# Gated linear attention in 128-token tiles: decays from the middle, three float32r products for states times query, states ahead of the gate, gate on feature partitions

## The chip, the cores and the metric

One core of one Trainium2 chip runs the whole program. The metric is the device time of one execution in microseconds; the kernel before was timed three times, and the median counts.

## What is computed

The reference is one inference step of a two-layer decoder: layer 0 has a recurrent mixer, layer 1 has gated linear attention (GLA); each layer then has cross-attention to a memory and an MLP. 1024 new tokens of one prompt and 8 sequences of 8 sample tokens go through it, 1088 token columns in all, everything in float32. The GLA mixer is the part that matters here. For each of 4 heads (key width 128, value width 256), with `bcum` the running sum of the log decays within a chunk:

```
q_in = qc * exp(bcum);  k_in = kc * exp(-bcum)
att  = where(mask, einsum('bthk,bshk->bhts', q_in, k_in), 0)
o    = einsum('bhts,bshv->bthv', att, vc) + einsum('bthk,bhkv->bthv', q_in, S)
k_end = kc * exp(g - bcum)
S    = exp(g) * S + einsum('bshk,bshv->bhkv', k_end, vc)
out  = (rmsnorm(o) * silu(gate)) @ w_out
```

The reference walks the prompt in chunks of 64 tokens; with another chunk length the result is the same apart from rounding. A sample sequence is one chunk of 8 tokens and starts from a given state.

## The kernel before

Activations lie transposed, features on partitions, in three column chunks c = 0, 1, 2 of 384, 384 and 320 columns (the last 64 are the samples). Each chunk has two or three 128-token tiles (`TILES`, `PTILES`). Every weight product splits both operands into a high and a low float32r part and issues three products into one PSUM bank (`mm3`, L97): that is the bulk of the program. PSUM has two banks under the name `pa`, three under `pb`, three under `pm`.

`gla` (L873) goes through the four heads one by one (L1099). `V` (L965) makes the values with tokens on partitions. Then for each chunk: `z_chain` (L930) makes the decays and their exponentials `qi`, `ki`, `ke`; `QK` (L974) makes queries and keys with features on partitions (`gemm_in`, L239) and multiplies them by those exponentials; `core_a` (L988) transposes `ke` into `kT` and makes the masked attention `att`; `G` (L1059) makes the gate with tokens on partitions (`gemm_tok`, L254); `core_b` (L1013) makes the output; `gate` (L1075) normalizes and gates it; `T` (L1086) transposes it, splits it into high and low parts and queues the output product (`gemm_out`, L266).

In `core_b` a 128-token tile holds two 64-token chunks. Each chunk has its own product of keys and values over 64 partitions (L1023), its own product of 64 queries with the state (L1030), and its own update of the state on VectorE (L1033), so that within a tile the second chunk's query product waits for the first one's update. The attention product covers the tile at once (L1027). These products are plain float32, and each stands in the trace as two TensorE instructions of 256 columns. In the last chunk the samples follow: the attention (L1040), eight query products with 32 columns of weights (L1051), eight products over 64 partitions for the new states (L1052), in pairs, with two buffers for the sample states and their loads (L1010) and stores (L1056).

The order on each engine is not the program's. A scheduler sets it when the kernel is compiled: it takes what is ready by its own clock, in order of priority, so that products of `QK` or of an output can stand between two products of `core_b`. On the chip every engine then keeps its compiled order.

## Time and profile before

| | us |
|---|---|
| three runs | 3103.0, 3103.41, 3107.08 |
| median | 3103.41 |
| profiled execution | 3104.66 |
| its span, first to last instruction | 3102.9 |
| TensorE busy in the span | 3050.6 |
| VectorE busy | 1743.2 |
| ScalarE busy | 1016.2 |

Busy time is the union of an engine's instructions. A matmul's record is longer than its turn, since matmuls are pipelined: the turn is the time from its start to the next one's start. The chain views give each piece of the path the time it held the path; the start column of a timeline gives the turns.

### The profile page before, as it was taken

How to read it: one execution, taken by the hardware profiler on the slowest of the kernel's cores; microseconds unless marked ns; L12 is line 12 of the kernel's file. 1: busy time of each engine (PE TensorE's matmuls, PEld its weight loads, DVE VectorE, ACT ScalarE, POOL GpSimd, SP SyncE). 2: the span in 40 equal slices, each digit the busy share in tenths (PEclk: the TensorE clock that was granted, in tenths of full speed). 3: DMA queues.
4: the chain of work that ended last, by engine and by line, in shares of the span. 5: the costliest groups of instructions: out<-in, count | busy, mean ns of one | idle time of the engine just before them, and what ended most of it. 6: DMA issues, size and time to landing. Idle time of an engine off the chain costs nothing.

```text
span 3102.9 us, 46542 instructions
## 1 busy us (share of the span) xinstructions
PE 3050.6 (98%) x19319; PEld 2930.7 (94%) x19319; DVE 1743.2 (56%) x3266; ACT 1016.2 (33%) x1847; POOL 193.6 (6%) x274
## 2 busy tenths in 40 slices
PE   8999999999999999999999999999999999999997
PEld 8999999989999999999889888899999999999997
DVE  7577786566444444446454454675575444444445
ACT  7555573234111211113333232442242112111114
POOL 4100020001000000001000000010010000000002
PEclk9999999999999999999999999999999999999998
DMA  8311113331111111111011102033321111111111
GB/s 271 119 43 43 42 60 103 102 113 36 54 42 42 55 42 41 46 50 43 28 57 42 57 28 70 21 98 106 126 62 55 42 41 48 48 42 41 45 51 58
DMA packets 155780, 194.85 MB, mean 63 GB/s; under 512 B 11281, under 2 KB 140561, under 8 KB 155569
## 3 DMA queue, kind: packets, MB, share of 16 engines
q1 hardware_dynamic: 152768, 182.82, 19.0%
q0 software_dynamic: 2800, 9.06, 0.8%
q8 instruction: 151, 2.47, 0.3%
q14 instruction: 61, 0.49, 0.1%
HBM read 178.34 MB, written 13.52 MB: 62 GB/s over the span
## 4 chain that ended last, share of the span: by engine, by line
PE 91%; DVE 4%; ACT 2%; DMA 2%; issue 1%; POOL 0%; SPq 0%; DVEq 0%; ACTq 0%; POOLq 0%
PE pa L101 12%; PE pa L99 12%; PE pa L100 12%; PE pb L99 9%; PE pb L100 9%; PE pb L101 9%; PE pm L99 5%; PE pm L100 5%; PE pm L101 4%; PE pa L262 2%; PE pa L264 2%; PE pa L263 2%; DVE xl L312 1%; DMA kvt<-in_cache_v 1%; PE pm L1030 1%
## 5 line engine op out<-in xcount | busy, mean ns | idle before, releaser
L100 PE MATMUL pa<-xl,whi 128*128 128x384 f32 (+2 forms) x2336 | 761.6, 326 | 2.7 <-DVE xl L312 2.7
L99 PE MATMUL pa<-xh,whi 128*128 128x384 f32 (+2 forms) x2336 | 761.5, 326 | 0.7 <-ACT xh L311 0.7
L101 PE MATMUL pa<-xh,wlo 128*128 128x384 f32 (+2 forms) x2336 | 761.9, 326 | 0.0
L279 DVE TENSOR_TENSOR x<-x,pb 128x384 f32<-128x384 f32 (+1 forms) x792 | 411.9, 528 | 206.7 <-PE pb L101 205.9
L99 PE MATMUL pb<-hh,whi 128*128 128x384 f32 (+1 forms) x1584 | 523.1, 332 | 4.5 <-DVE x L279 3.5
L100 PE MATMUL pb<-hl,whi 128*128 128x384 f32 (+1 forms) x1584 | 519.1, 328 | 0.0
L101 PE MATMUL pb<-hh,wlo 128*128 128x384 f32 (+1 forms) x1584 | 517.7, 327 | 0.0
L186 ACT CAST whi<-raw 128x1024 fp32r<-128x1024 f32 (+1 forms) x250 | 256.7, 1040 | 693.0 <-PE pa L100 349.2
L100 PEld LDWEIGHTS pa<-xl,whi 128*128 128x128 f32 x2336 | 439.3, 188 | 4.3 <-DVE xl L312 4.0
L99 PEld LDWEIGHTS pa<-xh,whi 128*128 128x128 f32 x2336 | 439.4, 188 | 2.7 <-ACT xh L311 1.0
L101 PEld LDWEIGHTS pa<-xh,wlo 128*128 128x128 f32 x2336 | 439.4, 188 | 0.6 <-DVE wlo L187 0.6
L187 DVE TENSOR_TENSOR wlo<-raw,whi 128x1024 fp32r<-128x1024 f32 (+1 forms) x250 | 303.3, 1224 | 241.0 <-ACT whi L186 240.2
L679 DVE SCALAR_TENSOR_TENSOR r<-pa,rstd 128x384 f32<-128x384 f32 (+1 forms) x192 | 102.4, 534 | 399.1 <-PE pa L101 398.4
L99 PEld LDWEIGHTS pb<-hh,whi 128*128 128x128 f32 x1584 | 297.5, 188 | 16.8 <-DVE x L279 7.2
L100 PEld LDWEIGHTS pb<-hl,whi 128*128 128x128 f32 x1584 | 298.2, 188 | 2.2 <-issue 1.6
L680 ACT ACTIVATE r<-r 128x768 f32<-128x768 f32 (+1 forms) x96 | 77.6, 808 | 674.4 <-DVE r L679 674.4
L101 PEld LDWEIGHTS pb<-hh,wlo 128*128 128x128 f32 x1584 | 298.0, 188 | 0.5 <-issue 0.4
L279 DVE TENSOR_TENSOR x<-x,pm 128x320 f32<-128x320 f32 (+1 forms) x360 | 191.0, 531 | 111.6 <-PE pm L101 111.5
L306 POOL TENSOR_TENSOR acc<-acc,sq 128x384 f32<-128x384 f32 (+1 forms) x105 | 118.8, 1132 | 2058.9 <-ACT sq L305 2040.3
L99 PE MATMUL pm<-hh,whi 128*128 128x320 f32 (+1 forms) x720 | 234.6, 326 | 0.0
L101 PE MATMUL pm<-hh,wlo 128*128 128x320 f32 (+1 forms) x720 | 234.5, 326 | 0.0
L100 PE MATMUL pm<-hl,whi 128*128 128x320 f32 (+1 forms) x720 | 234.5, 326 | 0.0
(305 smaller groups left out, 4338.7 us busy)
## 6 DMA issues: line engine op xcount, KB each, us to landing
raw<-in_mlp_w SPq DMA_DIRECT2D x128, 512.0 KB, 3.7
kvt<-in_cache_kT SPq DMA_DIRECT2D x64, 256.0 KB, 5.0
kvt<-in_cache_v SPq DMA_DIRECT2D x64, 256.0 KB, 4.8
raw<-in_xa_wv SPq DMA_DIRECT2D x16, 512.0 KB, 4.9
raw<-in_rg_w_in SPq DMA_DIRECT2D x16, 512.0 KB, 3.6
raw<-in_xa_wq SPq DMA_DIRECT2D x16, 512.0 KB, 3.4
raw<-in_xa_wo SPq DMA_DIRECT2D x16, 512.0 KB, 3.5
raw<-in_gla_w_in SPq DMA_DIRECT2D x16, 512.0 KB, 3.6
```

What stands on the lines that cost most here:

```text
L99: mm(out, lh, rh, start=first, stop=False)
L100: mm(out, lh, rl, start=False, stop=False)
L101: mm(out, ll, rh, start=False, stop=last)
L186: nc.scalar.copy(hi[:, o], raw[:, o])
L187: nc.vector.tensor_sub(lo[:, o], raw[:, o], f32(hi[:, o]))
L262: mm(out, self.xh[c][:, k, xs], hv[:, kk, :], start=k == 0, stop=False)
L263: mm(out, self.xh[c][:, k, xs], lv[:, kk, :], start=False, stop=False)
L264: mm(out, self.xl[c][:, k, xs], hv[:, kk, :], start=False, stop=k == 7)
L279: nc.vector.tensor_add(x, x, p[:, :per * w].rearrange("p (m t) -> p m t", m=per))
L306: (nc.vector if m % 4 == 3 else nc.gpsimd).tensor_add(self.acc[c][:, :w], self.acc[c][:, :w], sq[:, :w])
L679: nc.vector.scalar_tensor_tensor(r[:, f], p[f][:, :w], 0.0, self.rstd[c], op0=OP.max, op1=OP.mult)
L680: nc.scalar.activation(r, r, AF.Square)
```

## The change

A tile of 128 tokens becomes one chunk. The mask is a full lower triangle, and the prefix sums run over 128 tokens (three scans of 128 columns in place of one masked scan). The exponents of `qi` and `ki` are taken relative to the sum at the tile's 64th token; the state is multiplied by the decay up to there (`eg[:, i]`) before the query product, and by that of the whole tile (`eg[:, 4 + i]`) in its update. The query product uses high and low parts of the query (`qh`, `ql`, made in `core_a`) and of the scaled state (`sh`, `sl`), three float32r products per tile; the first tile of a head has no state and no such product. The key-value products, the state updates and the splits move to a new function `states`, which stands ahead of `G`. `G` uses `gemm_in` and so gives the gate with features on partitions; it is multiplied in behind the transposes in `T`, and `T` of the chunk before moves ahead of `G`. The samples' query products all stand ahead of their state products, and their states have four buffers, loaded at the start of the last chunk. `qi` has one buffer in place of two.

```diff
...
-            nc.vector.tensor_tensor_scan(bc[:, :pw], smask[:, :pw], m[:, :pw], 0.0, OP.mult, OP.add)
+            for t0 in range(0, pw, 128):
+                nc.vector.tensor_tensor_scan(bc[:, t0:t0 + 128], one, m[:, t0:t0 + 128], 0.0, OP.mult, OP.add)
...
+            nc.scalar.activation(eg[:, 0:n], bv[:, :, 63], AF.Exp, scale=1.0 / 16.0)
+            nc.scalar.activation(eg[:, 4:4 + n], bv[:, :, 127], AF.Exp, scale=1.0 / 16.0)
+            nc.vector.tensor_sub(view(d), bv, bv[:, :, 63:64].to_broadcast([128, n, 128]))
+            nc.scalar.activation(e[0][:, :pw], d[:, :pw], AF.Exp, scale=1.0 / 16.0)
+            nc.scalar.activation(e[1][:, :pw], d[:, :pw], AF.Exp, scale=-1.0 / 16.0)
+            d = self.t("tt", [128, MAXW], F32, 2)
+            nc.vector.tensor_sub(view(d), bv[:, :, 127:128].to_broadcast([128, n, 128]), bv)
...
+            qh = self.t("qih", [128, MAXW], R32)
+            ql = self.t("qil", [128, MAXW], R32)
+            nc.scalar.copy(qh[:, :pw], qi[:, :pw])
+            nc.vector.tensor_sub(ql[:, :pw], qi[:, :pw], f32(qh[:, :pw]))
...
-        def core_b(h, c, kT):
-            qi, ki, ke, eg = Z.pop(c)
-
-            kvs = {}
+        def states(c, kT):
+
+            eg, out = Z[c][3], []
             for i, (j, t0, tw) in enumerate(PTILES[c]):
                 if i % 2 == 0:
-                    bank = self.pa if i == 0 else self.pb
-                    two = [bank(), bank()]
-                kvs[i] = [t[:, i % 2 * 256:i % 2 * 256 + 256] for t in two]
-                for s in range(2):
-                    nc.tensor.matmul(kvs[i][s], kT[s * 64:s * 64 + 64, i, :], vo[j][s * 64:s * 64 + 64, :],
-                                     start=True, stop=True)
+                    bank = self.pb()
+                kv = bank[:, i % 2 * 256:i % 2 * 256 + 256]
+                nc.tensor.matmul(kv, kT[:, i, :], vo[j], start=True, stop=True)
+                if (c, i) == (0, 0):
+                    S["cur"] = self.t("S", [128, 256])
+                    nc.vector.tensor_copy(S["cur"], kv)
+                    out.append(None)
+                    continue
+                st = S["cur"]
+                sh, sl = self.t("Sh", [128, 256], R32, 2), self.t("Sl", [128, 256], R32, 2)
+                nc.scalar.activation(sh, st, AF.Copy, scale=eg[:, i:i + 1])
+                nc.vector.scalar_tensor_tensor(sl, st, eg[:, i:i + 1], f32(sh), op0=OP.mult, op1=OP.subtract)
+                nc.vector.scalar_tensor_tensor(st, st, eg[:, 4 + i:5 + i], kv, op0=OP.mult, op1=OP.add)
+                out.append((sh, sl))
+            return out
+
+        def core_b(h, c, kT, qh, ql, sts):
...
                 p = self.pm()
...
+                mm(o, atts[i], vo[j], start=True, stop=sts[i] is None)
+                if sts[i] is not None:
+                    sh, sl = sts[i]
+                    mm(o, qh[:, ts], sh, start=False, stop=False)
+                    mm(o, ql[:, ts], sh, start=False, stop=False)
+                    mm(o, qh[:, ts], sl, start=False, stop=True)
                 o_done(j, tw, p)
...
+            w = WID[c]
+            p = self.gemm_in(us, c)
             if c == NC - 1:
                 self.free(us)
-            return out
-
-        def gate(gss, c):
+            gt = self.t("gt", [128, 2, MAXW])
+            for f in range(2):
+                nc.vector.tensor_mul(gt[:, f, :w], p[f][:, :w], self.rstd[c])
+
+                sg = self.t("tt", [128, MAXW], F32, 2)[:, :w]
+                nc.scalar.activation(sg, gt[:, f, :w], AF.Exp, scale=-1.0)
+                nc.scalar.activation(sg, sg, AF.Ln, bias=1.0)
+                nc.scalar.activation(sg, sg, AF.Exp, scale=-1.0)
+                nc.vector.tensor_mul(gt[:, f, :w], gt[:, f, :w], sg)
+            return gt
...
-                nc.vector.scalar_tensor_tensor(vo[j][:tw], vo[j][:tw], ro[:tw, j:j + 1], gs[:tw], op0=OP.mult, op1=OP.mult)
...
+                nc.scalar.activation(vo[j][:tw], vo[j][:tw], AF.Copy, scale=ro[:tw, j:j + 1])
...
+                z = gt[:, dt, :w]
+                nc.vector.scalar_tensor_tensor(z, p[:, :w], gn, z, op0=OP.mult, op1=OP.mult)
+                nc.scalar.copy(hT[0][:, dt, :w], z)
+                nc.vector.tensor_sub(hT[1][:, dt, :w], z, f32(hT[0][:, dt, :w]))
...
-                    for b in range(0, 4, 2):
+                    for b in range(0, 8, 2):
                         load_s0(h, b)
-                kT = core_a(h, c)
+                core = core_a(h, c)
                 if c + 1 < NC:
                     z_chain(h, c + 1)
                     QK(us, h, c + 1)
                     self.tick()
+                if c:
+                    T(uo, h, c - 1, gt)
...
-                gss = G(ug, h, c)
+                sts = states(c, core[0])
+                gt = G(ug, h, c)
                 self.tick()
-                core_b(h, c, kT)
-                gate(gss, c)
+                core_b(h, c, *core, sts)
+                gate(c)
...
```

## Rows read from the trace of the kernel before

**Rows 1.** The page: busy us, share of the span and instructions of each engine.
```profile
PE 3050.6 (98%) x19319; PEld 2930.7 (94%) x19319; DVE 1743.2 (56%) x3266; ACT 1016.2 (33%) x1847; POOL 193.6 (6%) x274
```

**Rows 2.** GLA stretch: window, us, then busy us of PE, PEld, DVE, ACT, POOL; clock, DMA.
```profile
1467.00:2035.00 568.00, 563.34 (x3635) 485.53 (x3634) 296.50 (x655) 199.82 (x490) 35.82 (x49) 1.00 0.16 47
```

**Rows 3.** The longest wait of TensorE there: waiter, releaser, total us, times, longest.
```profile
PE pm L1030 <- DVE S L1033: 1.7, 3, 0.6
```

**Rows 4.** The chain that ended last in that stretch, shares of 568 us by line.
```profile
by line: PE pa L262 11.7%; PE pa L264 11.3%; PE pa L263 11.2%; PE pb L99 11.2%; PE pb L100 10.6%; PE pb L101 10.4%; PE pm L1030 5.0%; PE pa L1023 3.9%; PE pm L1027 3.2%; PE pa L1051 2.4%; PE pm L1052 1.8%; PE pm L938 1.7%; PE pm L995 1.7%;
```

**Rows 5.** The chain in one chunk's core: start us, us, what.
```profile
1541.64 0.84 PE pa L1023 x3
1542.48 0.11 PE pb L1023
...
1542.70 0.43 PE pb L1023 x3
1543.13 0.63 PE pm L1027 x2
1543.76 1.06 PE pa L1023 x4
...
1546.46 0.58 PE pm L1030 x2
1547.04 0.35 PE pb L99
```

**Rows 6.** Timeline of TensorE, float32r products, 256 columns, then 384: start us first.
```profile
1540.28 0.28 PE L264 MATMUL pa<-whi,xl 128*128 128x256 f32 x1
1540.40 0.28 PE L262 MATMUL pa<-whi,xh 128*128 128x256 f32 x1
...
1515.10 0.33 PE L99 MATMUL pb<-xh,whi 128*128 128x384 f32 x1
1515.28 0.33 PE L100 MATMUL pb<-xl,whi 128*128 128x384 f32 x1
1515.45 0.33 PE L101 MATMUL pb<-xh,wlo 128*128 128x384 f32 x1
```

**Rows 7.** Timeline of TensorE, float32 transposes among float32r products: start us first.
```profile
1607.69 0.28 PE L262 MATMUL pa<-whi,xh 128*128 128x256 f32 x1
1607.81 0.49 PE L1092 MATMUL pm<-ident,vo 128*128 128x128 f32 x3
1608.06 0.42 PE L100 MATMUL pb<-hl,whi 128*128 128x384 f32 x1
1608.32 0.34 PE L101 MATMUL pb<-hh,wlo 128*128 128x384 f32 x1
```

**Rows 8.** The chain in the sample part of the last head: start us, us, what.
```profile
2015.86 1.84 PE pa L1051 x8
2017.70 1.49 PE pm L1052 x6
...
2020.28 1.06 PE pm L1052 x4
...
2025.08 0.98 PE pa L1051 x4
```

**Rows 9.** VectorE and ScalarE in the stretch by line and shape: busy us, mean ns.
```profile
L1069 DVE SCALAR_TENSOR_TENSOR gs<-pa,rtok,gs 128x256 f32<-128x256 f32 x32 | 15.4, 483 | 43.2 <-ACT gs L1068 42.9
L1084 DVE SCALAR_TENSOR_TENSOR vo<-vo,oro,gs 128x256 f32<-128x256 f32 x32 | 15.2, 527 | 0.1
L1095 DVE SCALAR_TENSOR_TENSOR hl<-pm,vec,hh 128x384 fp32r<-128x384 f32 x16 | 9.9, 618 | 12.1 <-ACT hh L1094 12.1
L950 DVE TENSOR_TENSOR_SCAN tt<-smask,ki 128x384 f32<-128x384 f32 x8 | 7.7, 957 | 0.3
L957 DVE TENSOR_TENSOR tt<-tt 128x384 f32<-128x384 f32 x8 | 4.5, 558 | 0.3
L960 ACT ACTIVATE qi<-tt 128x384 f32<-128x384 f32 x8 | 4.1, 508 | 0.0
```

More of the change, by code (lines that the diff above doesn't have):

```diff
@@ L877, in gla @@
         w_in = a.gla_w_in[0]
-        smask = self.t("smask", [128, MAXW])
-        nc.gpsimd.memset(smask, 1.0)
-        nc.gpsimd.memset(smask.rearrange("p (n t) -> p n t", t=64)[:, :, 0], 0.0)
+        one = self.t("one", [128, 128])
+        nc.gpsimd.memset(one, 1.0)
         smask8 = self.t("smask8", [128, 64])
@@ L884, in gla @@
         nc.gpsimd.memset(smask8.rearrange("p (n t) -> p n t", t=8)[:, :, 0], 0.0)
-        ones = self.t("tt", [128, MAXW], F32, 2)[:, :128]
-        nc.gpsimd.memset(ones, 1.0)
         tri = self.t("tt", [128, MAXW], F32, 2)[:, :128]
-        nc.gpsimd.affine_select(tri, ones, pattern=[[1, 128]], compare_op=OP.is_ge, fill=0.0, base=0, channel_multiplier=-1)
-        nc.gpsimd.memset(tri[0:64, 64:128], 0.0)
+        nc.gpsimd.affine_select(tri, one, pattern=[[1, 128]], compare_op=OP.is_ge, fill=0.0, base=0, channel_multiplier=-1)
         pmask = self.t("pmask", [128, 128], U8)
@@ L894, in gla @@
         blk = self.t("blk", [64, 8])
-        nc.gpsimd.affine_select(blk, ones[:64, :8], pattern=[[-8, 8]], compare_op=OP.is_ge, fill=0.0, base=0, channel_multiplier=1)
+        nc.gpsimd.affine_select(blk, one[:64, :8], pattern=[[-8, 8]], compare_op=OP.is_ge, fill=0.0, base=0, channel_multiplier=1)
         nc.gpsimd.affine_select(blk, blk, pattern=[[8, 8]], compare_op=OP.is_ge, fill=0.0, base=7, channel_multiplier=-1)
@@ L916, in gla @@
         ro = self.t("oro", [128, 9])
-        ntok = self.t("ntok", [128, 9])
         def a_lo(c):
@@ L954, in z_chain @@
             d = self.t("tt", [128, MAXW], F32, 2)
-            for t0, n, L, g0 in ((0, PRO[c] // 64, 64, 0),) + (((256, 8, 8, 4),) if c == NC - 1 else ()):
-                bv = bc[:, t0:t0 + n * L].rearrange("p (n t) -> p n t", t=L)
-                nc.vector.tensor_sub(d[:, t0:t0 + n * L].rearrange("p (n t) -> p n t", t=L),
-                                     bv[:, :, L - 1:L].to_broadcast([128, n, L]), bv)
-                nc.scalar.activation(eg[:, g0:g0 + n], bv[:, :, L - 1], AF.Exp, scale=1.0 / 16.0)
@@ L960, in z_chain @@
-            nc.scalar.activation(e[0][:, :w], bc, AF.Exp, scale=1.0 / 16.0)
-            nc.scalar.activation(e[1][:, :w], bc, AF.Exp, scale=-1.0 / 16.0)
+            n = pw // 128
+            bv = bc[:, :pw].rearrange("p (n t) -> p n t", t=128)
+            view = lambda ap: ap[:, :pw].rearrange("p (n t) -> p n t", t=128)
+            nc.scalar.activation(eg[:, 0:n], bv[:, :, 63], AF.Exp, scale=1.0 / 16.0)
+            nc.scalar.activation(eg[:, 4:4 + n], bv[:, :, 127], AF.Exp, scale=1.0 / 16.0)
@@ new lines, in z_chain @@
+            nc.vector.tensor_sub(view(d), bv, bv[:, :, 63:64].to_broadcast([128, n, 128]))
[3 more added lines that the diff above has]
+            nc.vector.tensor_sub(view(d), bv[:, :, 127:128].to_broadcast([128, n, 128]), bv)
+            if c == NC - 1:
+                sv = bc[:, pw:w].rearrange("p (n t) -> p n t", t=8)
+                nc.vector.tensor_sub(d[:, pw:w].rearrange("p (n t) -> p n t", t=8), sv[:, :, 7:8].to_broadcast([128, 8, 8]), sv)
+                nc.scalar.activation(eg[:, 8:16], sv[:, :, 7], AF.Exp, scale=1.0 / 16.0)
+                nc.scalar.activation(e[0][:, pw:w], bc[:, pw:w], AF.Exp, scale=1.0 / 16.0)
+                nc.scalar.activation(e[1][:, pw:w], bc[:, pw:w], AF.Exp, scale=-1.0 / 16.0)
@@ L1038, in core_b @@
                 nc.gpsimd.dma_start(a.S_prompt[0, 0, h], S.pop("cur"))
-                po = self.pa()
-                nc.tensor.matmul(po[:64, :256], att8, vo[8][:64, :], start=True, stop=False)
+                po = self.pm()
+                mm(po[:64, :256], att8, vo[8][:64, :], start=True, stop=False)
+                for b in range(8):
+                    g = b // 4 * 32
+                    mm(po[g:g + 32, :256], qm[:, b, :], s0s[b // 2 * 2][:, b % 2, :], start=False, stop=b % 4 == 3)
                 for b in range(0, 8, 2):
-                    if b not in s0s:
-                        load_s0(h, b)
                     s0 = s0s.pop(b)
@@ L1059, in G, with gate @@
         def G(us, h, c):
-            out = []
-            for j, t0, tw in TILES[c]:
-                p = self.pa()
-                self.gemm_tok(us, c, t0, tw, p[:tw, :256])
-                gs = self.t("gs", [128, 256], F32, 3)
-                nc.scalar.activation(gs[:tw], p[:tw, :256], AF.Exp, scale=ntok[:tw, j:j + 1])
-                nc.scalar.activation(gs[:tw], gs[:tw], AF.Ln, bias=1.0)
-                nc.scalar.activation(gs[:tw], gs[:tw], AF.Exp, scale=-1.0)
-                nc.vector.scalar_tensor_tensor(gs[:tw], p[:tw, :256], self.rtok[:tw, j:j + 1], gs[:tw], op0=OP.mult, op1=OP.mult)
-                out.append(gs)
+            w = WID[c]
+            p = self.gemm_in(us, c)
             if c == NC - 1:
                 self.free(us)
-            return out
-        def gate(gss, c):
+            gt = self.t("gt", [128, 2, MAXW])
[7 more added lines that the diff above has]
+            return gt
+        def gate(c):
             j0 = TILES[c][0][0]
```

51 lines of the change are left out of this document (17 added, 34 removed).

## The prediction

> **What bounds the kernel now.** I read the page first, then the busy times of the GLA stretch, its waits, its chain, and last the timelines that give the price of one turn. TensorE is busy for 3050.6 of 3102.9 us [rows 1]. In the 568 us in which this mixer runs it is busy for 563.3 us at the full clock (1.00), while VectorE is busy for 296.5 and ScalarE for 199.8 [rows 2]: 4.7 us of TensorE's time are idle there. The waits say the same from the other side: the longest, that of the query products for the state update, is 1.7 us in total [rows 3]. So there is hardly a stall to remove. What the change can win is TensorE's own work, and the chain of the stretch shows who holds the path: the query products (L1030) 5.0% of 568 us, the key-value products (L1023) 3.9% in `pa` alone, the attention products (L1027) 3.2% [rows 4].
>
> **Prices of a turn.** A float32 pass of 256 columns: six take 1.49 us, four 1.06 [rows 8], so 0.215 us each; a run of n passes that takes up half or a quarter of the array costs 0.215 n plus 0.20 (1.06 less 4 times 0.215). The same 0.20 stands on a run of two full-array passes that comes behind half-array ones (0.63 for two L1027) [rows 5], so it is paid at each change of shape. The next float32r product behind such a run holds the path for 0.35 us instead of 0.17 [rows 5]: 0.18 for the way back. A float32r product costs 0.12 us with 256 columns and 0.173 with 384 (two starts in 0.35) [rows 6]; with 320 I put 0.147, between them.
>
> **The change part by part**, on TensorE, over four heads.
>
> - Core of the prompt. Before: L1030 28.4 us (5.0% of 568), L1023 22.2 in `pa` plus 32 passes in `pb` at 0.135 (0.11 and 0.43 for four [rows 5]), 4.3, L1027 18.2 [rows 4]: 73.1. After: the key-value products of whole tiles are 8 per head, 64 passes, at 0.215: 13.8. The attention products stay 64 passes; without the changes of shape they cost 13.8. The query products are 28 tiles with three float32r products at 0.12: 10.1. Sum 37.7, a gain of 35.4.
> - Gate. Before, 9 tiles of 24 products at 0.12: 25.9 us per head. After, 48 products in each chunk, 48 times (0.173 + 0.173 + 0.147): 23.7. Four heads: 8.8 gained. The sum counts turns alone, as all these products are full tiles of float32r.
> - Samples. The 128 passes (64 query, 64 state) stay. In the last head they stand in runs of 8, 6, 4 and 4 [rows 8], with two more; with the query products together there should be three or four. I take four runs less per head, 16 times 0.20: 3.2 gained. The loads of states b = 4 and 6, which waited for a buffer, go out with the first two; two more issues stand on SP's queue ahead of weight loads. Their cover is the last chunk's `G` (48 turns of 0.147, 7 us) and the output product popped ahead of it (8.3 us); without it a weight unit that comes late would be waited for, a few us a head at most.
> - Products between the pieces of the core. Twelve times a float32r product followed a half-array one of the core; at 0.18 [rows 5] that is 2.2 gained.
> - Waits: the 1.7 us for the state update [rows 3] go, since `states` makes all updates while `G` runs. What is late next is the third pair of `sh`, `sl`: the middle chunk needs three pairs and has buffers for two. The third is made once the first tile's products are done, in a ScalarE step of 256 columns (0.51 with 384, so some 0.42) and a VectorE step of 0.48 [rows 9] plus hand-over, some 1.2 us by estimate; the cover is the second tile (0.43 + 0.36) and the third's attention product (0.43), 1.22. I put 0.3 us a head, 1.2 in all; without any cover it would be 4.8.
> - Switches from float32 passes to float32r within a tile, 56 of them. The trace has none of two-pass products in the full array. The nearest rows are transposes among float32r products: no time is lost on the way in (0.12), and three of 128 columns with the product behind them take 0.51 us [rows 7] where 3 times 0.108 (half of 0.215) and 0.173 make 0.50. So I take 0.01 each, 0.6. The other end is the 0.20 of a change of shape: 11.
> - VectorE, per chunk of 384: scans about +0.3 (by estimate: three starts in place of one, on 0.957), one more subtraction for the exponents and one for `ql` at 0.56, two for the split in `T` at 0.56, four in `G` at 0.56 in place of three at 0.48, and three gate products of 0.53 less [rows 9]: +1.8, so some 21 us in all. ScalarE: +0.5 for `qh`, some 0.42 a tile for `sh` and again for the gate's scale, a small exponential, and six of 0.51 in `G` for nine of some 0.43 (256 columns, by estimate): +2.3, some 27 us. In a stretch of about 518 us that makes VectorE 61% and ScalarE 44% busy [rows 2]. I cost it at nothing: the cover is the 8.3 us of turns in each of `QK` and `G`. Longest is `z_chain`: with three exponentials, two VectorE steps, a scan, two subtractions and three more exponentials it takes about 7 us [rows 9], and it must be done when `QK` of the same chunk is. With the cover gone it would be paid in part twelve times (the slower rival).
> - POOL loses a memset per head and four small ones in the setup; nobody waits for them. At nothing.
> - Leftover: 1 us for waits that I do not see.
>
> Gains 35.4 + 8.8 + 3.2 + 2.2 + 1.7 = 51.3; costs 1.2 + 0.6 + 1.0 = 2.8; net 48.5. The profiled execution took 3104.66 us, its span and 1.8 us around it, which is 1.25 above the median of the runs. Against it the sum gives 3056; from the median of 3103.4 it gives 3055, which is my number.
>
> **A rule against it.** The rows of one core show key-value passes of the two halves both ways: four in line in 1.06 us, and others whose turns fall to 0.11 because two run side by side [rows 5]. Page "TensorEngine Tiling (Array Packing)" of the Trainium skill, section Key Properties, says that tiles on different parts of the array load and multiply in parallel, by which the two halves before would already cost no more than one whole product. By that rule, joining them would gain only the changes of shape. By these rows the overlap is the exception, and the chain's share is what was paid; the sum goes by it, and the rule is a rival.
>
> **The rivals.**
>
> 1. *The halves ran together.* If the path's share of L1023 holds other work's time, joining halves wins little: 26.5 us before against 13.8 after, so up to 12.7 less gain. For it: turns of 0.11; against: four passes in 1.06 [rows 5]. It gives 3068. Chance 0.08.
> 2. *Buffers give part back.* `qi`, `gt` and the split state have few buffers, `tt` two for eight uses a chunk, and `T` now stands between `QK` and `G` and needs the gate's scale first. If each of twelve chunks loses 1.5 us on this, 18 us go back: 3073. For it: more steps in series on VectorE and ScalarE; against: TensorE found 563.3 us of work in 568 [rows 2] with similar chains, since the compiled order fills gaps. Chance 0.16.
> 3. *The three products are not what they say.* If the query products ran as float32 passes, 84 of them would cost 0.43 instead of 0.12: 26 us back, 3081. Against it: the same type gives 0.12 in `V` [rows 6]. Chance 0.02.
> 4. *Slower: the single `qi` buffer puts `z_chain` on the path.* The next chunk's `qi` may be written only when attention, `qh`, `ql` and, in the last chunk, a POOL copy have read the old one. If the chain of some 7 us then begins only at the end of `QK`, its banks stay full and TensorE stands still. It decides from 48.5 / 12 = 4 us a chunk; fully exposed it is 12 times 7, 84 us: 3139. Against it: only the two last exponentials need `qi` and `ki` free, and 8.3 us of `QK` lie over the chain. Chance 0.03.
>
> **How the numbers follow.** The forecast has 0.71, with its own range 3042 to 3066: the lower end adds another 13 us, as much again as the 7 us of the smaller gains and 6 for changes of shape around other products that I did not count; the upper end takes the 11 us of switches. Rivals 1 and 2 reach to 3073, with some spread to 3078; the range 3042 to 3078 leaves out less than 2 in 10. About 0.2% (6 us) is what a measurement of this kernel can tell from no change. Faster by more than that: forecast and rivals 1 to 3, less a little for a mixture of 2 and 3 that eats nearly everything: 0.95. Within it: 0.02. Slower: 0.03.
>
> **What would show it.** Right: in the GLA stretch (then about 520 us) the chain gives the key-value, attention and state-query products together about 38 us, the state-query products turn over every 0.12 us, the gate's products stand at 0.173, and TensorE's idle time stays under some 8 us. Wrong: float32r products of the core at 0.2 or more apart (the switches), waits of TensorE for `sl`, `gt` or `qi` of more than 10 us in total (rival 2), or the query and key banks waiting for exponentials (rival 4). The prediction falls if the stretch gets shorter by less than 30 us.

## The result and the profile after

The changed kernel takes 3050.45 us (median of four runs, 3049.25 to 3050.82) beside 3105.24 for the kernel before (3103.0 to 3107.08; in the later comparisons its medians are 3103.3 to 3105.4). The ratio is 0.9823 with a 95% interval of 0.9806 to 0.984: faster by 1.8%. The forecast was 3055.0 in 3042 to 3078. The profiled execution took 3050.53 us, its span is 3048.8; against the profiled execution before (3104.66) that is a gain of 54.1 us where 48.5 were forecast.

The page of the changed kernel: busy us, share of the span and instructions of each engine, beside [rows 1].

```profile
PE 2999.3 (98%) x18923; PEld 2920.6 (96%) x18923; DVE 1752.6 (57%) x3304; ACT 1038.8 (34%) x1907; POOL 193.6 (6%) x267
```

TensorE has 51.3 us and 396 instructions less; VectorE has 9.4 us more and ScalarE 22.6 us more, and neither is near its limit.

Where it went is told by cutting the execution at the same two places in each kernel: from the start of the first value product of the GLA mixer (L262) to the start of the last transpose of its gated output. For the kernel before and then the kernel after, the windows between these places: window, us, busy us of PE, PEld, DVE, ACT, POOL; clock, DMA share and GB/s.

```profile
1466.78:2036.45 569.67, 564.80 (x3644) 486.67 (x3642) 298.17 (x659) 200.71 (x491) 36.46 (x50) 1.00 0.16 47
```

```profile
1464.88:1980.41 515.53, 511.81 (x3246) 475.06 (x3244) 308.67 (x697) 223.70 (x552) 38.74 (x42) 1.00 0.17 52
```

The stretch is 569.67 - 515.53 = 54.1 us shorter, which is the whole gain: without it the profiled executions leave 3104.66 - 569.67 and 3050.53 - 515.53, 2535.0 us each. TensorE's idle time in it is 515.53 - 511.81 = 3.7 us, 4.9 before. The granted clock is 1.00 in both, the upper of its two levels (2.4 GHz). What lies outside the stretch is untouched by the edits and still takes 2529.7 to 2535.6 us in the profiled executions, while the stretch of the same kernel run again came out at 515.51. So the experiments below are read by their stretch, cut at the same two places, with the total beside it.

The waits of TensorE in the stretch after (waiter, releaser, total us, times, longest), beside [rows 3]:

```profile
PE pm L1001 <- DVE ke L994: 1.6, 3, 0.5
PE pb L99 <- DVE x L279: 0.9, 1, 0.9
PE pb L1033 <- DVE S L1036: 0.7, 3, 0.2
PE pb L1033 <- DVE S L1043: 0.3, 1, 0.3
```

The wait of the query products for the state update is gone. New is a wait of the transposes of `ke` (L1001), 1.6 us.

Pieces of the chain after (start us, us, what): key-value products of a whole chunk, one tile of the core and the end of its chunk, and the sample part of the first head, beside [rows 5] and [rows 8].

```profile
1531.11 0.18 PE pb L101
1531.28 0.86 PE pb L1033 x4
1532.14 0.18 PE pa L99
...
1562.81 0.43 PE pm L1053 x2
1563.24 0.12 PE pm L1056
1563.36 0.12 PE pm L1057
1563.48 0.12 PE pm L1058
...
1565.05 0.28 PE pm L1058
...
1585.14 0.57 PE pm L1063 x2
1585.72 2.74 PE pm L1066 x16
1588.45 1.92 PE pb L1074 x8
```

Four key-value passes take 0.86, which is 4 times 0.215, and the product behind them 0.18: in the full array a float32 run costs nothing that the chain shows, on the way in or back. One tile is 0.43 for the attention (L1053) and 0.12 for each of the three query products: 0.79 us, with nothing lost at the switch of type. The middle chunk's third L1058, which needs the third pair of `sh`, `sl`, holds the path for 0.28 instead of 0.12: at most 0.16 a head goes to that pair. The sixteen query passes of the samples (L1066) stand in one run of 2.74, less than 16 times 0.215, 3.44.

The turns of TensorE in the stretch, summed by what the product is for (each turn from a product's start to the next one's start, us):

| products | before | after | gained |
|---|---|---|---|
| key-value | 26.50 | 10.24 | 16.3 |
| attention (samples' one included) | 20.73 | 10.90 | 9.8 |
| queries times state | 28.81 | 16.16 | 12.7 |
| values and gate (L262 to L264, and L99 to L101 into `pa`) | 217.10 | 209.27 | 7.8 |
| output (L99 to L101 on `h`) | 103.28 | 100.09 | 3.2 |
| samples: queries | 15.58 | 10.95 | 4.6 |
| samples: new states | 17.66 | 15.37 | 2.3 |
| transposes in `T` | 6.94 | 8.69 | -1.7 |
| queries and keys (L99 to L101 into `pb`), with the waits in them | 98.24 | 99.51 | -1.3 |
| the rest | 34.83 | 34.35 | 0.5 |
| sum | 569.67 | 515.53 | 54.1 |

A turn that ends at a change of kind can be booked on either side of it. The key-value products show 64 turns in 10.24 us, though 64 passes at 0.215 are 13.8. The product behind a run starts 0.03 us after the run's last pass and then keeps its turn for 0.37 us instead of 0.17 (start us, us, what):

```profile
1531.12 1.02 PE L1033 MATMUL pb<-vo,kT 128*128 128x256 f32 x4
1531.79 0.53 PE L99 MATMUL pa<-xh,whi 128*128 128x384 f32 x1
1532.16 0.34 PE L100 MATMUL pa<-xl,whi 128*128 128x384 f32 x1
```

There are 24 such products behind the key-value runs, all in the row of values and gate. So some 3.5 us of key-value products stand in that row: put back, the key-value products gain 12.7 and values and gate 11.3. Sums over neighbouring rows are free of this.

### The profile page after: what moved, and what is told of

It reads as the page before. It is cut to its first block, busy times and chain, and to the rows that moved or that the text cites. A ratio compares the mean times of both kernels' runs of the same rounds, so it can differ in the third digit from the quotient of the medians.

```text
span 3048.8 us, 45853 instructions
## 1 busy us (share of the span) xinstructions
PE 2999.3 (98%) x18923; PEld 2920.6 (96%) x18923; DVE 1752.6 (57%) x3304; ACT 1038.8 (34%) x1907; POOL 193.6 (6%) x267
## 4 chain that ended last, share of the span: by engine, by line
PE 91%; DVE 4%; ACT 2%; DMA 1%; issue 1%; POOL 0%; DVEq 0%; SPq 0%; ACTq 0%; POOLq 0%
PE pa L101 13%; PE pa L99 13%; PE pa L100 13%; PE pb L99 9%; PE pb L101 9%; PE pb L100 9%; PE pm L99 5%; PE pm L100 5%; PE pm L101 5%; PE pa L262 1%; DMA kvt<-in_cache_v 1%; PE pa L263 1%; PE pa L264 1%; DVE xl L312 1%; PE pb L800 1%
## 5 line engine op out<-in xcount | busy, mean ns | idle before, releaser
L99 PE MATMUL pa<-xh,whi 128*128 128x384 f32 (+2 forms) x2528 | 827.1, 327 | 0.7 <-ACT xh L311 0.7
L100 PE MATMUL pa<-xl,whi 128*128 128x384 f32 (+2 forms) x2528 | 825.1, 326 | 2.7 <-DVE xl L312 2.7
L101 PE MATMUL pa<-xh,wlo 128*128 128x384 f32 (+2 forms) x2528 | 827.4, 327 | 0.0
L279 DVE TENSOR_TENSOR x<-x,pb 128x384 f32<-128x384 f32 (+1 forms) x792 | 412.4, 528 | 209.4 <-PE pb L101 208.5
L99 PE MATMUL pb<-hh,whi 128*128 128x384 f32 (+1 forms) x1584 | 525.2, 332 | 3.2 <-DVE x L279 2.2
L101 PE MATMUL pb<-hh,wlo 128*128 128x384 f32 (+1 forms) x1584 | 519.6, 328 | 0.0
L100 PEld LDWEIGHTS pa<-xl,whi 128*128 128x128 f32 x2528 | 475.7, 188 | 4.6 <-DVE xl L312 3.9
L99 PEld LDWEIGHTS pa<-xh,whi 128*128 128x128 f32 x2528 | 475.8, 188 | 2.6 <-ACT xh L311 1.0
L101 PEld LDWEIGHTS pa<-xh,wlo 128*128 128x128 f32 x2528 | 475.6, 188 | 1.0 <-DVE wlo L187 0.7
L99 PEld LDWEIGHTS pb<-hh,whi 128*128 128x128 f32 x1584 | 299.0, 189 | 13.2 <-DVE x L279 6.6
L101 PEld LDWEIGHTS pb<-hh,wlo 128*128 128x128 f32 x1584 | 298.7, 189 | 0.1
L279 DVE TENSOR_TENSOR x<-x,pm 128x320 f32<-128x320 f32 (+1 forms) x360 | 190.9, 530 | 111.7 <-PE pm L101 111.6
L99 PE MATMUL pm<-hh,whi 128*128 128x320 f32 (+1 forms) x720 | 234.8, 326 | 0.0
L101 PE MATMUL pm<-hh,wlo 128*128 128x320 f32 (+1 forms) x720 | 234.8, 326 | 0.0
```

The source lines that it names most:

```text
L99: mm(out, lh, rh, start=first, stop=False)
L100: mm(out, lh, rl, start=False, stop=False)
L101: mm(out, ll, rh, start=False, stop=last)
L279: nc.vector.tensor_add(x, x, p[:, :per * w].rearrange("p (m t) -> p m t", m=per))
```

## The experiments

Each starts from the changed kernel, unless it says from which other one. All compute the whole of the reference's output.

### The change again, and the gate alone

`a0_after` is the changed kernel once more.

> The changed kernel once more, so that the kernels of this call stand beside it on one chip. Turns theory (the gain is TensorE's own turns): 3050 us, with the same 515 us in the GLA stretch. If the 6 us by which it beat the forecast were a matter of the chip it ran on, it comes out at 3055 or more here.

Measured: 3050.49 us (3045.74 to 3051.15), ratio 0.9823 (0.9809 to 0.9838), stretch 515.51. The gain comes out again, and the stretch repeats to 0.02 us.

`e1_gate_tok` puts the old gate back, tokens on partitions, with the old `gate` and `T`, and keeps the rest of the change:

```diff
-            p = self.gemm_in(us, c)
+            for j, t0, tw in TILES[c]:
+                p = self.pa()
+                self.gemm_tok(us, c, t0, tw, p[:tw, :256])
...
-                nc.scalar.activation(vo[j][:tw], vo[j][:tw], AF.Copy, scale=ro[:tw, j:j + 1])
+                nc.vector.scalar_tensor_tensor(vo[j][:tw], vo[j][:tw], ro[:tw, j:j + 1], gs[:tw], op0=OP.mult, op1=OP.mult)
```

> The gate's product with tokens on partitions again (and its scaling in front of the transposes), all else as in the changed kernel. Turns theory: four heads lose 8.8 us (576 turns of 0.173, 0.173 and 0.147 become 864 of 0.12), so 3059. Rival (the gate's new place pays because its banks come free sooner, after one VectorE step in place of four steps): TensorE also waits for the banks, over 5 us of waits on the gate's steps, and 3064 or more. Second rival (the longer steps of the split behind the transposes cost as much as the turns win): no difference, 3050.

Measured: 3055.87 us (3054.62 to 3058.87). Its stretch, and two of its waits:

```profile
1467.01:1988.49 521.48, 517.35 (x3527) 481.86 (x3525) 305.53 (x697) 219.97 (x548) 34.35 (x41) 1.00 0.17 51
```

```profile
PE pm L1002 <- DVE ke L995: 1.6, 3, 0.5
PE pm L1115 <- DVE vo L1107: 0.5, 1, 0.5
```

The stretch is 521.48 - 515.53 = 5.95 us longer. The turns of values and gate are back at 217.12, so the gate's own products were worth 7.85 us where the forecast had 8.8; the transposes go from 8.69 down to 6.79, so 1.9 of that had been paid back in `T`. The only wait on a step of the gate is 0.5 us for `vo` (L1107, 0.2 in the changed kernel), and the wait for `ke` is the same 1.6: the turns decide here and not the gate's buffers or its steps on VectorE.

### The samples' order

`e3_sample_pairs` puts the samples' query products back among their state products, with the four buffers kept:

```diff
-                for b in range(8):
-                    g = b // 4 * 32
-                    mm(po[g:g + 32, :256], qm[:, b, :], s0s[b // 2 * 2][:, b % 2, :], start=False, stop=b % 4 == 3)
                 for b in range(0, 8, 2):
...
+                        g = (b + i) // 4 * 32
+                        mm(po[g:g + 32, :256], qm[:, b + i, :], s0[:, i, :], start=False, stop=(b + i) % 4 == 3)
                         mm(p[:, i * 256:i * 256 + 256], km[:, i, :], vo[8][:64, :], start=True, stop=True)
```

> The samples' eight query products stand in pairs among the state products again; four buffers and early loads stay. Turns theory as forecast (only changes of array shape count, four a head at 0.20): 3.2 us lost, 3053.5. Rival (query products of the two column groups run side by side when they stand together: sixteen took 2.74 us where 16 times 0.215 and 0.20 would be 3.64): another 0.9 us a head is lost, some 7 us in all, 3057.

Measured: 3056.28 us (3054.89 to 3058.13), stretch 524.71, longer by 9.2. The chain in its first head's samples (start us, us, what; L1072 queries, L1073 states):

```profile
1583.43 0.55 PE pm L1072 x2
1583.98 0.63 PE pb L1073 x2
...
1588.13 1.84 PE pm L1072 x8
```

Each single product, two passes, holds the path for 0.55 or 0.63: 0.43 and a change of shape of 0.12 to 0.20. Its queries take 16.39 us and its states 18.67, together 8.7 more than after. There are 11 runs in this head and in the next two, and 12 in the last, where the changed kernel has 3 in each; 33 more at 0.12 to 0.20 make 4.0 to 6.6 us. The rest, 2.6 at least, is what the next experiment shows.

`e4_sample_alt` only changes the order of the eight query products, so that neighbours lie in different groups of 32 output partitions (samples 0 to 3 in one, 4 to 7 in the other):

```diff
-                for b in range(8):
+                for b in (0, 4, 1, 5, 2, 6, 3, 7):
```

> The samples' query products alternate between the two column groups (samples 0, 4, 1, 5, ...). If neighbours in different column groups run side by side, the sixteen passes take about 8 times 0.215 and 0.20, 1.9 us in place of 2.74, and four heads win 3.3 us: 3047. Rival (passes that write one PSUM bank take turns whatever the group, and the 2.74 us came of something else): 2.7 to 3.6 us a head as before or worse, 3050 to 3054.

Measured: 3045.9 us (3041.67 to 3046.26), ratio 0.9809 (0.9794 to 0.9823), stretch 511.96, shorter by 3.6. The chain at the same place as above:

```profile
1582.80 0.57 PE pm L1063 x2
1583.38 1.85 PE pm L1066 x16
```

The same sixteen passes take 1.85 instead of 2.74: eight times 0.215 and 0.13. The passes start in pairs 6 to 7 ns apart. So two passes on different column groups (groups of 32 output partitions) run side by side when the order alternates between the groups. In the changed kernel's run the starts in the trace show four passes alone, then four pairs 6 to 31 ns apart, then four passes alone: part of the overlap is there already. In the program's order the two groups meet at one place only, so, if the compiled order is the same, passes need not be direct neighbours for it; how far apart they may stand was not tried. Against 16 times 0.215 and the 0.20 of a change of shape, 3.64, the 2.74 are 0.90 us less a head, 3.6 over four heads. A run of eight query passes before took 1.84 [rows 8], all in line.

### The core: type, and halves

`e2_query_f32` makes the query product one float32 product per tile and drops the low parts (`ql`, `sl`):

```diff
-            nc.vector.tensor_sub(ql[:, :pw], qi[:, :pw], f32(qh[:, :pw]))
...
-                nc.vector.scalar_tensor_tensor(sl, st, eg[:, i:i + 1], f32(sh), op0=OP.mult, op1=OP.subtract)
...
-                    mm(o, qh[:, ts], sh, start=False, stop=False)
-                    mm(o, ql[:, ts], sh, start=False, stop=False)
-                    mm(o, qh[:, ts], sl, start=False, stop=True)
+                    mm(o, qh[:, ts], sh, start=False, stop=True)
```

> The state-query product as one float32 product per 128-token tile; the low parts of query and state and the three float32r products are gone. Turns theory (the gain is the whole tile, hardly the type): 28 tiles times 0.43 less 0.36, 2 us lost in the chain of the stretch, 3052; VectorE loses two steps a tile, which hides nothing and gains nothing. Rival (the type is what pays, as float32 in this place takes its turns and changes of mode as before): the query products go back towards 28.8 us, 10 us or more lost, 3060.

Measured: 3046.9 us (3045.18 to 3048.29), ratio 0.9816 (0.9798 to 0.9833), stretch 513.70, shorter by 1.8 where it should have become longer by about 2. The price of the products came as forecast: attention and queries take 29.25 us instead of 27.06, 2.2 more. But the products of queries and keys take 96.98 instead of 99.51, and the wait for `ke` in this kernel is

```profile
PE pm L1001 <- DVE ke L994: 0.2, 1, 0.2
```

VectorE shows one part of it. The place of the first of these waits (in the second head) in the changed kernel and then in `e2_query_f32`, whose stretches start within 0.01 us of each other (start us, us, what; in brackets the idle time before it and its releaser):

```profile
1645.02 0.56 DVE L1011 TENSOR_TENSOR qil<-qi,qih 128x384 fp32r<-128x384 f32 x1 [0.58 <-ACT qih L1010]
1645.50 0.55 DVE L992 TENSOR_TENSOR tt<-pb,rstd 128x384 f32<-128x384 f32 x1
...
1646.56 0.55 DVE L994 TENSOR_TENSOR ke<-ke,tt 128x384 f32<-128x384 f32 x1
1647.16 0.33 PE L1001 MATMUL pm<-ident,ke 128*128 128x128 f32 x1 [0.54 <-DVE ke L994]
```

```profile
1644.97 0.56 DVE L992 TENSOR_TENSOR tt<-pb,rstd 128x384 f32<-128x384 f32 x1
...
1646.04 0.55 DVE L994 TENSOR_TENSOR ke<-ke,tt 128x384 f32<-128x384 f32 x1
1646.64 0.33 PE L1001 MATMUL pm<-ident,ke 128*128 128x128 f32 x1
```

In the changed kernel the subtraction for `ql` (L1011), which itself waits 0.58 us for ScalarE's copy, stands ahead of the steps that make `ki` and `ke`; L992 then starts 0.53 us later and `ke` comes 0.52 us later, with TensorE's transposes waiting for it. This is one of three such places, whose waits sum to 1.6; in the first head, where nothing waits, `ke` comes only 0.07 later. The key-value products' wait for `S` (L1036), 0.7, is gone too, and TensorE's idle time falls from 3.7 to 1.4 us in all. That is 2.3 of the 4.0 us by which the rest of the stretch is shorter; the other 1.7 are not traced to a wait, and the compiled order is another one in this kernel. So the three float32r products are cheaper on TensorE, but with the split that they need the stretch is longer; that the split's steps cost more than the products save is shown for 2.3 us against 2.2, and argued for the rest.

`e9_query_halves`, from `e2_query_f32`, computes the query product in two halves of 64 queries, as before the change, but with the same state for both:

```diff
-                    mm(o, qh[:, ts], sh, start=False, stop=True)
+                    for s in range(2):
+                        mm(o[s * 64:s * 64 + 64], qh[:, t0 + s * 64:t0 + s * 64 + 64], sh, start=False, stop=True)
```

> As the float32 query product, but in two halves of 64 queries, both with the same state: the shape of before without its waits. Turns theory (halves in line, and a change of shape before and behind): 28 tiles times 0.43 more and 0.2 to 0.4 for the shapes, 17 to 23 us over the whole-tile float32 product, about 3070. Rival (halves on different column groups run side by side): 0.2 to 0.4 us a tile for the shapes alone, 6 to 11 us over it, about 3060.

Measured: 3053.74 us (3052.47 to 3055.11), stretch 520.73, 7.0 longer than `e2_query_f32`. Attention and queries take 36.75 us, 7.5 more. The chain (L1051 attention, L1055 the two halves):

```profile
1541.28 0.86 PE pm L1051 x4
1542.14 0.58 PE pm L1055 x4
1542.72 0.63 PE pm L1051 x2
1543.35 0.58 PE pm L1055 x4
```

Four half-array passes take 0.58, not 4 times 0.215 and 0.20 = 1.06; their starts are 6 to 7 ns apart in pairs. The halves run side by side, and what they cost is the change of shape, in and back: 7.5 / 28 = 0.27 us a tile. So the halves as such were not what the 28.81 us of query products before consisted of. There the second half had another state, and in the trace of the kernel before 26 of the 64 halves stand alone, each for 0.58 us (two passes and a change of shape); of the 19 runs that hold two halves, 12 ran side by side already and 4 in part.

`e5_kv_halves` makes the key-value product in two halves of 64 tokens again, each into its own bank, with one more addition on VectorE:

```diff
-                nc.tensor.matmul(kv, kT[:, i, :], vo[j], start=True, stop=True)
+                for s, o in enumerate((kv, kw)):
+                    nc.tensor.matmul(o, kT[s * 64:s * 64 + 64, i, :], vo[j][s * 64:s * 64 + 64, :], start=True, stop=True)
...
+                nc.vector.tensor_add(st, st, kw)
```

> The key-value product of a tile in two halves of 64 partitions into two banks, as before, with an addition on VectorE; all else as changed. Turns theory (halves mostly in line, as the forecast took them): 32 products of 0.43 more and shapes at 0.2 each way for some 20 runs, 16 to 22 us lost, 3066 to 3072. Rival (first rival of the forecast: halves on different row groups run side by side, so joining them won only the shapes): 4 to 8 us, 3054 to 3058.

Measured: 3072.61 us (3071.48 to 3075.31), ratio 0.9901 (0.9884 to 0.9919), stretch 539.35, longer by 23.8. The key-value products take 33.44 us instead of 10.24. The chain (L1034 the halves):

```profile
1532.00 1.13 PE pb L1034 x4
1533.13 0.38 PE pa L99
...
1534.03 0.63 PE pb L1034 x2
1534.65 0.37 PE pa L100
```

Here four passes take 1.13, in line, and single halves that stand among the gate's products take 0.63 each, with 0.37 for the product behind where 0.18 is usual. Of the 32 products, 13 have their two halves apart in the compiled order; 8 run side by side (16 of the 128 passes start within 10 ns of the one before); the other 11 stand together and overlap in part or not at all. 1.7 us of the loss are waits of these products for their banks (L992, L279). Why 11 that stand together do not overlap, where all 28 of `e9_query_halves` (on different output partitions, in one bank) did, was not taken apart. What is shown is that undoing this part costs more than undoing any other part tried. It is not what the part won: these halves take 33.44 us, those of the kernel before took 26.50.

### What stands where

`e6_states_late` moves `states` behind the gate's products:

```diff
-                sts = states(c, core[0])
                 gt = G(ug, h, c)
                 self.tick()
+                sts = states(c, core[0])
                 core_b(h, c, *core, sts)
```

> The key-value products, state updates and splits stand behind the gate's product in the program, straight ahead of the core. Theory (the place ahead of the gate is what covers the chain of updates): a chunk's first query product now waits for key-value product, update and split, about 0.4 + 0.5 + 0.5 us and more for the later tiles, less what the compiled order finds to put between: 0.5 to 1.5 us in each of twelve chunks, 3056 to 3068. Rival (the scheduler fills any order with other products): within 2 us of 3050.

Measured: 3047.85 us (3045.32 to 3049.23), ratio 0.9821 (0.9808 to 0.9834), stretch 515.05, which is 0.5 less. Key-value products and gate together take 112.5 us instead of 114.0 here, attention and queries 30.6 instead of 27.1, the other rows 2.5 less; the wait for the scaled state is 0.3. The place of `states` in the program is worth nothing that shows: the compiled order puts the products among others from either place.

`e12_ql_pool` moves the subtraction for `ql` from VectorE to POOL, which was nearly idle:

```diff
-            nc.vector.tensor_sub(ql[:, :pw], qi[:, :pw], f32(qh[:, :pw]))
+            nc.gpsimd.tensor_sub(ql[:, :pw], qi[:, :pw], f32(qh[:, :pw]))
```

> The subtraction that makes the low part of the query runs on POOL in place of VectorE; all else as changed. Theory (on VectorE it stands ahead of the last steps of the keys, which TensorE then waits for, 1.6 us in three of four heads): those waits go, 1.6 us shorter in the stretch, 3049. Rival (the float32 query kernel is shorter for another reason: fewer products that take a turn each, or the split of the state): no change, 3050.5.

Measured: 3047.92 us (3046.1 to 3050.16), ratio 0.9823 (0.9809 to 0.9836), stretch 514.73, shorter by 0.8. The wait for `ke` should have gone and did not; it rose:

```profile
PE pm L1001 <- DVE ke L994: 2.1, 3, 0.7
```

The timeline at one such place:

```profile
1643.08 0.56 DVE L993 TENSOR_TENSOR ki<-ki,tt 128x384 f32<-128x384 f32 x1
1643.09 1.41 POOL L1011 TENSOR_TENSOR qil<-qi,qih 128x384 fp32r<-128x384 f32 x1 [49.10 <-ACT qih L1010]
1643.55 1.36 DVE L994 TENSOR_TENSOR ke<-ke,tt 128x384 f32<-128x384 f32 x1
1644.97 0.44 PE L1001 MATMUL pm<-ident,ke 128*128 128x128 f32 x2 [0.69 <-DVE ke L994]
```

The subtraction takes 1.41 on POOL, and the step for `ke` (L994) beside it takes 1.36 us instead of 0.55. It starts at 1643.55 and ends at 1644.91, 0.41 after POOL's step is over (1643.09 + 1.41 = 1644.50), as if it had stood until then. This is so in three heads; in the other chunks of this width the step takes 0.55, and POOL's subtraction takes 1.01 where no such step stands beside it. So, counted from the start of the stretch, `ke` comes only 0.08 us earlier here than with `ql` on VectorE, though L992 starts 0.9 us earlier. The theory is borne out for L992; that the wait would then go is not shown by this run. That VectorE and POOL hold each other up is what page "SBUF — State Buffer" of the Trainium skill, section "SBUF: two separate sides", says of a VectorE operation with two inputs in SBUF and a POOL operation that reads SBUF: one holds the shared ports for its whole instruction and the other stands. The trace agrees, with the 0.55 that became 1.36.

### Versions beyond the change

`e10_alt_both`, from `e4_sample_alt`, gives each sample's state product over 32 partitions instead of 64 and lets neighbours alternate between the two groups:

```diff
-                        mm(p[:, i * 256:i * 256 + 256], km[:, i, :], vo[8][:64, :], start=True, stop=True)
+                        for g in range(2):
+                            r = slice(g * 32, g * 32 + 32)
+                            mm(banks[g][:, i * 256:i * 256 + 256], kms[g][r, i, :], vo[8][r, :], start=True, stop=True)
```

> On the kernel with alternating query products, the samples' state products too: each over the 32 partitions of its four samples, neighbours on different row groups and in different banks. If row groups run side by side as column groups do, 16 passes a head fall from 3.84 us (15.37 over four heads) to some 2.0: 7 us less than the alternating kernel, 3039, and 12 less than the changed one. Rival (row groups take turns, or VectorE's updates of the states become the bound): 3046.

Measured: 3043.08 us (3042.73 to 3046.12), ratio 0.9806 (0.979 to 0.9821), stretch 511.00, 1.0 less than `e4_sample_alt`. The chain at one group, and the wait of these products:

```profile
1590.62 0.34 DVE km L1071
1591.01 1.46 PE pb L1078 x8
```

```profile
PE pb L1078 <- DVE km L1071: 2.8, 3, 1.8
```

These eight passes, the second group of their head, take 1.46 where they took 1.92 in line. The first group stands right behind the query products (start us, us, what):

```profile
1585.99 1.13 PE L1078 MATMUL pb<-vo,km 32*128 32x256 f32 x8
1587.05 0.39 PE L262 MATMUL pa<-whi,xh 128*128 128x256 f32 x1
```

It takes 1.06, which is 4 times 0.215 and a change of shape of 0.20, and its passes start 6 to 7 ns apart in pairs, in all four heads. So on input partitions too the groups run side by side. The samples' state products take 9.73 us instead of 15.37. But TensorE now waits 2.8 us for `km` (L1071), since two of its buffers must be ready at a time; the value products ahead, which hold these waits as their turns, take 3.0 us more, and output products 1.4. 5.6 us won on the spot leave 1.0.

`e11_best` joins `e2_query_f32` and `e10_alt_both` and gives `km` four buffers.

```diff
-                        km = self.t("km", [64, 2, 128], F32, 2)
+                        km = self.t("km", [64, 2, 128], F32, 4)
```

> Three findings together: the state-query product as one float32 product, the samples' query products alternating between column groups, their state products alternating between row groups with four buffers for the masked keys. If the three add up: GLA stretch 513.7 (float32 query) less 3.5 (query products) less some 7 (state products side by side, no wait for masked keys), 503 us, total 3036 to 3037. Rival (VectorE's updates of the sample states bound that part): the state products are waited for, stretch 507 or more, total 3040 or more.

Measured: 3048.05 us (3047.24 to 3052.09), ratio 0.9826 (0.9813 to 0.984), stretch 512.40. The parts do not add, and the rival that the expectation names is what came. The wait for `km` is gone and the next stands in its place:

```profile
PE pb L1074 <- DVE s L1078: 3.3, 4, 1.6
```

Now TensorE waits until VectorE's updates of the sample states (L1078) have read the banks. The state products take 16.46 us again, with the first group of each head side by side and the second in line behind gaps of 0.8 to 1.9 us. Behind the samples' state products there is VectorE's own time, and a faster TensorE there only waits longer.

`e13_f32_alt` joins the two parts that had no such wait, `e2_query_f32` and the order of `e4_sample_alt`.

> The two findings that each shortened the GLA stretch without a new wait, together: the state-query product as one float32 product per tile, and the samples' query products alternating between column groups. If they add up: stretch 515.5 less 1.8 less 3.5, 510.2 us, and some 3044 in all. Rival (as when three were put together, a new wait on VectorE takes it back): stretch 512 or more and 3047.

Measured: 3043.57 us (3042.85 to 3045.04), ratio 0.9803 (0.979 to 0.9816). Its stretch, and all that TensorE waits for in it for 0.3 us or more:

```profile
1464.31:1974.57 510.26, 508.99 (x3212) 470.81 (x3211) 292.19 (x657) 221.49 (x552) 36.04 (x42) 1.00 0.17 52
```

```profile
PE pb L99 <- DVE x L279: 0.9, 1, 0.9
PE pb L1032 <- DVE S L1041: 0.3, 1, 0.3
```

The stretch is 510.26: 515.53 less 1.83 and 3.57, the gains of the two alone, is 510.13. The parts add. It is the shortest stretch of all, TensorE is idle in it for 1.3 us, and it computes with less VectorE work than the change. Its total is 0.9803 of the kernel before (3105.44 beside it), which the totals do not tell from the 0.9806 of `e10_alt_both` and the 0.9809 of `e4_sample_alt`. Every one of its runs lies below every run of the changed kernel (the fastest 3045.74), though those stood beside other runs of the kernel before.

## Why the prediction was right, by its own steps

The forecast named the right bound and the right mechanism: TensorE's turns, with hardly a wait to remove. What it said would show it is there: the stretch of 515.5 us beside "about 520", in its chain 37.0 us for the three products of the core beside "about 38" (key-value 12.6, attention 13.9, queries 10.5), float32r turns of 0.12 in it, 3.7 us idle beside "under some 8". Its terms beside the measured ones, with the 3.5 us of key-value products put back into the core:

| term | forecast | measured | read from |
|---|---|---|---|
| core, with the wait for the state, third pair and switches: 35.4 + 1.7 - 1.2 - 0.6 | 35.3 | 35.2 | key-value, attention, query turns: 38.7, less 3.5 |
| gate | 8.8 | 7.85 | `e1_gate_tok` |
| products between pieces of the core | 2.2 | 6.7 | value, gate and output turns: 7.8 + 3.2 + 3.5, less the gate |
| samples | 3.2 | 6.9 | the two sample rows |
| leftover | -1.0 | -2.5 | transposes -1.7, queries and keys -1.3, rest +0.5 |
| sum | 48.5 | 54.1 | |

So the 5.6 us beyond the forecast are 4.5 from the products between the pieces and 3.7 from the samples, less 1.0 at the gate, 1.5 in the leftover and 0.1 at the core.

**Core.** The step was right, and its net size too. The attention row holds the samples' attention, 2.29 us before and after alike. Without it the core's turns are 73.8 before, where the shares of the chain [rows 4] and the wait gave 73.1 + 1.7 = 74.8, and 38.5 after with the 3.5 put back, where 37.7 + 1.2 + 0.6 = 39.5 were expected: both sides lie 1.0 lower, and that this cancels is luck. The three prices held: 0.215 a pass, 0.12 a float32r product, 0.79 a tile.

**Costs of it.** The third pair cost at most four times 0.16, 0.6, instead of 1.2. The switches were put at 0.6 and cost nothing that the chain shows; their other end of 11 us is out.

**Products between the pieces.** This term was mis-sized: 2.2 against 6.7. It counted twelve float32r products behind the core's half-array pieces, and only the way back. In the trace before, 24 float32r products stand right behind a half-array piece, 12 of them behind the samples', and hold 2.5 us beyond their usual turns (0.12, 0.146 and 0.174 for 256, 320 and 384 columns); 40 stand right ahead of one and hold some 4.0 more. After the change 1.1 of these 6.5 us are left, beside the samples' pieces.

**Samples.** This term was mis-sized too: 3.2 against 6.9. The step priced every pass in a run at 0.215 and counted only the changes of shape that went. It failed where it said that the 128 passes "stay": in one run some lie side by side, which is worth 3.6 us over four heads, nearly all of the difference. `e3_sample_pairs` undid the order and lost 9.2 us; `e4_sample_alt` changed only which passes are neighbours and won 3.6. Page "TensorEngine Tiling (Array Packing)" of the Trainium skill, section Key Properties, which the prediction quoted against the joining of the halves, is borne out here by the 1.85 us for sixteen passes, and in the changed kernel it works for the change; on the halves of the key-value products in `e5_kv_halves` it is borne out for 8 products of 32.

**Gate.** Right in kind, 1.0 too large on the products (8.8 against 7.85); the 1.9 that the transposes in `T` cost had no term. Why these take longer was not tried.

**VectorE at nothing.** The cover hides nearly all of it. What got through is the subtraction for `ql` ahead of the steps for `ke`: 1.4 of the 1.6 us of TensorE's wait go with the split (`e2_query_f32`), and so do 0.7 of the 1.0 us that the key-value products wait for the state's steps. The prediction named `z_chain` as the long chain; what got onto the path was an extra step of 0.56, with a wait of its own for ScalarE, in front of another one. So of the change's parts the float32r split is worth nothing here: it loses 1.8 us. Nor does the place of `states` win anything (`e6_states_late`).

**The rivals.** The first (the halves ran together, 3068) is out by the total, and by the key-value products' own gain: 26.5 before against 13.8 after, the 12.7 that it would have taken back. `e5_kv_halves` points the same way: with halves they cost 23.2 us more. For the query products its mechanism is true (`e9_query_halves`), at 0.27 us a tile. The second (few buffers give 18 us back) has 1.6 us for `ke`, which no buffer causes, and 1.0 of the key-value products for the state's steps (L1036, L1043); `e1_gate_tok` took out `gt` and the gate's steps and left the wait for `ke` as it was. The third is out by 0.12 us a turn. The fourth, slower, is out: no wait for `qi` or the exponentials is in the list, and TensorE is idle for 3.7 us in all.

## What to carry to other kernels

When TensorE is busy for 99% of a stretch, price a change in turns by shape, and then look at the order of neighbours: here passes on different column groups of the array cost one turn for two when the order alternated between the groups, and with the groups in blocks only four pairs of eight did; one line of order won 3.6 us, while the split into three cheaper products lost 1.8. A step that TensorE saves must be weighed against the place of what it needs on VectorE, not against VectorE's busy share. Before moving such a step to POOL, ask what VectorE does beside it.

## What the runs showed of the hardware that was not expected

Float32 passes on different groups of output partitions start 6 to 7 ns apart and cost one turn of 0.215 for two; sixteen took 1.85 us alternating, 2.74 in two blocks. On groups of input partitions the same was seen (eight passes in 1.06, right behind the query products) and also in part or hardly at all (eight in 1.46, four halves of 64 partitions in 1.13). In the full array a switch between float32 and float32r costs nothing that the chain shows: 0.86 for four passes and 0.18 behind them, where it cost 0.35 behind half-array passes [rows 5]. And a two-input step of VectorE with 384 columns went from 0.55 to 1.36 us beside a POOL subtraction of 1.41.
